# A hybrid decoder block on one core: the running sums of W_down's quarters, built in DRAM by two queues behind the weight loads

## The chip, the cores and the metric

One core of one Trainium2 chip runs the whole block. The metric is the device time of one execution in microseconds (us); lower is better. Engines: PE multiplies matrices, DVE, ACT and POOL work on vectors, SP only issues transfers. POOL can issue transfers too. A transfer issued by SP goes to the queue that the profile calls q1 (hardware), one issued by POOL to q0 (software).

## The reference, cut to what matters

```python
h = rmsnorm(x, norm_mix_pre)                                # x: 512 tokens x 1024
gq, gk, gv, gg1, gr, pu, mq, mk, mv, gates = split(h @ w_in)
ya = gla_mixer(gq, gk, gv, gg1, gr, ...) @ w_branch_a       # gated linear attention
yb = pool_mixer(pu, ...) @ w_branch_b
yc = moba_mixer(mq, mk, mv) @ w_branch_c                    # block-sparse attention
x = x + rmsnorm((sigmoid(gates) . (ya, yb, yc)) @ w_out)
h = rmsnorm(x, norm_ffn_pre)
f = (silu(h @ ffn_w_gate) * (h @ ffn_w_up)) @ ffn_w_down    # ffn_w_down: 2816 x 1024
x = x + rmsnorm(f)
```

## The kernel before

All products are made in split precision: every operand is kept as a high and a low part, and three matmuls stand for one (`mm_fm`, L212, and `mm_tm`, L221). A weight is fetched by `load` (L167) in chunks of 512 KB. `split_chunk` (L160) puts one chunk into a buffer `raw` (three of them, `NRAW`), issued by SP (L163); ACT then casts it into the high part (L164), DVE subtracts for the low part (L165), which frees the buffer. The high and the low part have four buffers each.

The order of work: the four row tiles of x are normalised and transposed, and the projection `g1r` (gate rank and half of the output gate) is done tile by tile, in an order written out by hand for DVE, ACT and PE (L370 to L423). Then come GLA's queries and keys (`gq`, `gk`), the decay, GLA's values (`gv`), the second half of the output gate (`gr`), GLA's chunks; MoBA in two halves (`mv`, `mq`, `mk`, scores and values), with the gates and the branch product `a` between; the pooling branch `b` (`pu`); branch `c`; `w_out` with its norms; the feed-forward matrices; and last the product with W_down (`product`, L930). Everything outside the hand-written stretch is put in order by a scheduler that works on a simulated timeline, with the chunks of `load` drawn ahead by a priority of 400. On its engine each instruction runs in the order so fixed, and a waiting one holds those behind it.

The last product is done by a scheme with seven products of quarters in place of eight. Four of its right-hand sides are sums of quarters of W_down. They are weights alone and are made by the transfer engines, DRAM to DRAM: for each sum, six plain copies (`sums[t, n]` from a quarter, or from an earlier sum) and six transfers that add a second quarter to it. There are 24 copies and 24 adding transfers, 512 KB each apart from four of 256 KB in either set. `background` (L149) hands out one of these 48 at each `load` other than those of `gq` and `gk`, all on POOL's queue. They have nothing to wait for but each other, so the scheduler places them as early as POOL is free. The sums are read from 777 us on.

```python
def background():
    for t, first, second in ((1, (0, 0), (0, 1)), (3, (1, 1), (0, 1)), (2, 1, (1, 1)), (4, 2, (1, 0))):
```

POOL has little else: a square root step `rs_m` for each row tile (L254), one subtraction for `g1r` (L352), clearing of buffers, some steps of GLA (L632, L636) and of MoBA (L704, L713), and the sums over the branches (L807).

Of the kernel before, what the change touches and what calls it, by code (L numbers as in the profile page):

```python
# [13 lines left out]
ALU = mybir.AluOpType  # L14
AX = mybir.AxisListType

P = 128
# [58 lines left out]
def hybrid_block(ctx: ExitStack, tc: tile.TileContext, a: dict, out: bass.AP):  # L76
    nc = tc.nc
# [16 lines left out]
    def slot(shape, name, dt=F32):  # L94
        n = int(np.prod(shape[1:]))
        if n > D or dt != F32:
            i = free_full.pop(0)
            owner[name] = (i, None, 0)
            return big.tile(shape, dt, tag=f"S{i}", name=name, bufs=1)
        if free_half:  # L100
            i, t, lo = free_half.pop(0)
        else:
            i, lo = free_full.pop(0), 0
            t = big.tile([P, 2 * D], F32, tag=f"S{i}", name=f"two_{name}", bufs=1)
            free_half.append((i, t, D))
        owner[name] = (i, t, lo)
        ap = t[:, lo:lo + n]
        names = "abcd"[:len(shape) - 1]
        if len(shape) > 2:
            ap = ap.rearrange(f"p ({' '.join(names)}) -> p {' '.join(names)}",  # L110
                              **{c: k for c, k in zip(names, shape[1:])})
        return ap
# [26 lines left out]
    chunks = [(lo, min(lo + 2, KH)) for lo in range(0, KH, 2)]  # L139

    def wq(z, c, lo, hi):

        r = (z * KH + lo) * P
        return wd[r:r + (hi - lo) * P, c * T:(c + 1) * T]

    sums = {(t, n): dram.tile([(hi - lo) * P, T], F32, name=f"sum{t}_{n}")
            for t in (1, 2, 3, 4) for n, (lo, hi) in enumerate(chunks)}

    def background():  # L149
        for t, first, second in ((1, (0, 0), (0, 1)), (3, (1, 1), (0, 1)), (2, 1, (1, 1)), (4, 2, (1, 0))):  # L150
            for n in range(len(chunks)):
                src = sums[first, n] if type(first) is int else wq(*first, *chunks[n])
                yield nc.gpsimd.dma_start(sums[t, n], src)
            for n in range(len(chunks)):
                yield nc.gpsimd.dma_start(sums[t, n], wq(*second, *chunks[n]), accum_op=ALU.add)

    behind = background()


    def split_chunk(src, kt, nf, H, L, name, eng, lead):  # L160
        with tc.high_priority(offset=lead):
            raw = wpool.tile([P, kt, nf], F32, tag="raw", name=f"raw_{name}", bufs=NRAW)
            nc.sync.dma_start(raw, src.rearrange("(k p) f -> p k f", p=P))  # L163
            S.copy(H, raw)  # L164
            (eng or V).tensor_tensor(L, raw, H.bitcast(F32), op=ALU.subtract)  # L165

    def load(src, name, eng=None, lead=LEAD, keep=False):  # L167


        if not name.startswith(("gq", "gk")):  # L170
            next(behind, None)
        K, nf = src.shape[0] // P, src.shape[1]
        kt = 4 if nf == G1W else D // nf
        out = []
        for c in range(K // kt):
            if keep:
                HL = slot([P, 2, kt, nf], f"{name}_{c}", F32R)
                h, l = HL[:, 0], HL[:, 1]
            else:
                h = wpool.tile([P, kt, nf], F32R, tag="wH", name=f"wH_{name}_{c}", bufs=NWH)  # L180
                l = wpool.tile([P, kt, nf], F32R, tag="wL", name=f"wL_{name}_{c}", bufs=NWH)
            split_chunk(src[c * kt * P:(c + 1) * kt * P, :], kt, nf, h, l, f"{name}_{c}", eng, lead)
            out.append((h, l, c * kt, kt))
        return out

    class Pair:
# [125 lines left out]
    raw = [wpool.tile([P, 4, G1W], F32, tag="raw", name=f"raw_g1r{c}", bufs=NRAW) for c in range(2)]  # L312
# [57 lines left out]
    with tc.manual_schedule(engines={E.DVE, E.Activation, E.PE}):  # L370
# [50 lines left out]
        for pair in ("HH", "HL", "LH"):  # L421
            for c in range(2):
                st_mm(3, c, pair)  # L423
    wgq = load(w_in[:, C_GQ:C_GQ + 256], "gq", None, 0)
    wgk = load(w_in[:, C_GK:C_GK + 256], "gk", None, 0)
    for t in range(NT):
        free(f"x_{t}", f"hn{t}")
# [43 lines left out]
    gq, gk = gqk[:, 0], gqk[:, 1]  # L471

    def proj_tm(dst, c, name):
        W = load(w_in[:, c:c + 256], name)
        for tp in range(2):
            ps = acc(f"{name}_{tp}")
            for j in range(2):
                mm_tm(ps[:, j * 256:(j + 1) * 256], hT, 2 * tp + j, W, 0, 256)
            dst(2 * tp, ps.rearrange("p (t f) -> p t f", t=2))
# [11 lines left out]
    for i in range(2):  # L491
        for j in range(2):
            t = 2 * i + j
# [110 lines left out]
    for c in range(NT):  # L604
        ob = side(f"o{c}")
        up = side(f"up{c}") if c < NT - 1 else None
        for p in range(2):
            n = p * 4 + c
# [7 lines left out]
        if c < NT - 1:  # L616
            for p in range(2):
                n = p * 4 + c
# [290 lines left out]
    for u in range(NF // 2):  # L909
# [5 lines left out]
        for f in range(2):  # L915
            k = 2 * u + f
# [148 lines left out]
```

## Time and profile before

| | |
|---|---|
| time, median of 3 runs | 871.37 us (870.96 to 877.25) |
| time of the profiled execution | 871.97 us |
| its span in the trace | 870.2 us |
| PE busy | 824.5 us, 95% of the span |
| DVE busy | 455.6 us, 52% |
| ACT busy | 327.0 us, 38% |
| POOL busy | 97.3 us, 11% |
| mean granted clock of PE | 0.988 |

The time of the profiled execution is its span and 1.8 us around it. A busy PE is one with a matmul in its pipeline; matmuls overlap, so that one of 512 columns lasts some 0.39 us in the rows but follows the one before by 0.23 us at the full clock.

### The profile page before, as it was taken

To read this page: it belongs to the slowest core of one execution; us is meant where nothing else is said; L and a number is where in the kernel's file an instruction comes from. 1 tells how busy PE (TensorE), PEld (TensorE's weight loads), DVE (VectorE), ACT (ScalarE), POOL (GpSimd) and SP (SyncE) were. 2 spreads that over 40 slices of the span, in tenths; PEclk is the share of its full clock that TensorE was granted. 3 is DMA by queue.
4 is the path that set the end of the run, shared out by engine and by line. 5 is a ranking of instruction groups with operands and counts; after the bars stand their busy time and mean duration, and the time that the engine had idled before them with its cause. 6 is when DMAs were issued, how large, how long until landed. Compare 5 with 4: busy or idle time off the path is not lost.

```text
span 870.2 us, 10358 instructions
## 1 busy us (share of the span) xinstructions
PE 824.5 (95%) x4082; PEld 698.6 (80%) x4082; DVE 455.6 (52%) x674; ACT 327.0 (38%) x496; POOL 97.3 (11%) x109
## 2 busy tenths in 40 slices
PE   0389989999999999999999999999999999999996
PEld 0387889888988887788888889888888888888885
DVE  1262978676647665443345563323232434586655
ACT  2144342455536542222334343222222222365543
POOL 4452300111100100121121110000000000000001
PEclk9989999999999999999999999999999999999998
DMA  8999992223132263143324242333333333268673
GB/s 289 293 236 307 275 219 74 74 72 96 51 98 82 64 201 110 52 121 97 96 97 146 97 144 76 97 96 97 97 97 97 96 98 96 85 201 284 193 210 129
DMA packets 82386, 118.39 MB, mean 136 GB/s; under 512 B 4305, under 2 KB 58338, under 8 KB 82146
## 3 DMA queue, kind: packets, MB, share of 16 engines
q1 hardware_dynamic: 74338, 94.67, 35.5%
q0 software_dynamic: 8000, 23.07, 10.9%
q8 instruction: 32, 0.52, 0.3%
q14 instruction: 16, 0.13, 0.0%
HBM read 113.53 MB, written 27.26 MB: 162 GB/s over the span
## 4 chain that ended last, share of the span: by engine, by line
PE 89%; DMA 6%; DVE 2%; SPq 1%; issue 1%; ACT 1%; DVEq 0%; POOLq 0%; POOL 0%; ACTq 0%
PE ff L218 28%; PE p L947 12%; PE pga L218 5%; PE pgb L218 5%; PE ow L229 5%; PE pgc L218 5%; DMA raw_gq<-in_w_in_dram 4%; PE gqk L218 3%; PE mv L229 3%; PE pya L218 3%; PE pu L218 3%; PE mq L218 3%; PE pyb L218 3%; PE mk L218 3%; PE pyc L218 3%; DMA raw_mv<-in_w_in_dram 2%
## 5 line engine op out<-in xcount | busy, mean ns | idle before, releaser
L218 PE MATMUL ff<-h2L,wH_ffn_w_gate 128*128 128x512 f32 (+1 forms) x192 | 71.3, 372 | 0.0
L218 PE MATMUL ff<-h2L,wH_ffn_w_up 128*128 128x512 f32 (+1 forms) x192 | 71.3, 372 | 0.0
L218 PE MATMUL ff<-h2H,wL_ffn_w_up 128*128 128x512 f32 (+1 forms) x192 | 71.3, 372 | 0.0
L218 PE MATMUL ff<-h2H,wL_ffn_w_gate 128*128 128x512 f32 (+1 forms) x192 | 71.2, 371 | 0.0
L218 PE MATMUL ff<-h2H,wH_ffn_w_gate 128*128 128x512 f32 (+1 forms) x192 | 71.2, 372 | 0.0
L218 PE MATMUL ff<-h2H,wH_ffn_w_up 128*128 128x512 f32 (+1 forms) x192 | 71.1, 371 | 0.0
L165 DVE TENSOR_TENSOR wL_ffn_w_gate<-raw_ffn_w_gate,wH_ffn_w_gate 128x1024 fp32r<-128x1024 f32 x22 | 26.9, 1225 | 78.9 <-ACT wH_ffn_w_gate L164 78.7
L939 DVE TENSOR_TENSOR wL_p<-raw_p,wH_p 128x1024 fp32r<-128x1024 f32 (+1 forms) x42 | 47.2, 1133 | 30.9 <-ACT wH_p L938 30.7
L938 ACT CAST wH_p<-raw_p 128x1024 fp32r<-128x1024 f32 (+1 forms) x42 | 41.1, 980 | 52.4 <-PE p L947 22.4
L947 PE MATMUL p<-wH_p,qs 128*128 128x512 f32 x176 | 54.7, 390 | 0.3 <-ACT two_s L1001 0.3
L165 DVE TENSOR_TENSOR wL_ffn_w_up<-raw_ffn_w_up,wH_ffn_w_up 128x1024 fp32r<-128x1024 f32 x22 | 26.9, 1225 | 41.8 <-ACT wH_ffn_w_up L164 41.7
L164 ACT CAST wH_ffn_w_up<-raw_ffn_w_up 128x1024 fp32r<-128x1024 f32 x22 | 23.2, 1053 | 68.1 <-issue 35.3
L164 ACT CAST wH_ffn_w_gate<-raw_ffn_w_gate 128x1024 fp32r<-128x1024 f32 x22 | 23.2, 1053 | 61.0 <-PE ff L218 53.1
L254 POOL TENSOR_TENSOR rs_pf<-ms_pf,half 128x1 f32<-128x1 f32 x4 | 3.4, 840 | 340.8 <-DVE ms_pf L252 340.8
L218 PEld LDWEIGHTS ff<-h2L,wH_ffn_w_up 128*128 128x128 f32 x192 | 36.2, 188 | 6.3
L218 PEld LDWEIGHTS ff<-h2L,wH_ffn_w_gate 128*128 128x128 f32 x192 | 36.2, 188 | 6.3
L218 PEld LDWEIGHTS ff<-h2H,wH_ffn_w_gate 128*128 128x128 f32 x192 | 36.1, 188 | 6.3
L218 PEld LDWEIGHTS ff<-h2H,wH_ffn_w_up 128*128 128x128 f32 x192 | 36.1, 188 | 6.3
L218 PEld LDWEIGHTS ff<-h2H,wL_ffn_w_gate 128*128 128x128 f32 x192 | 36.2, 188 | 6.2
L218 PEld LDWEIGHTS ff<-h2H,wL_ffn_w_up 128*128 128x128 f32 x192 | 36.2, 188 | 6.1
L947 PE MATMUL p<-wH_p,a 128*128 128x512 f32 x132 | 41.0, 389 | 0.0
L947 PEld LDWEIGHTS p<-wH_p,qs 128*128 128x128 f32 x176 | 33.0, 188 | 7.6 <-ACT two_s L1001 0.7
(335 smaller groups left out, 2089.4 us busy)
## 6 DMA issues: line engine op xcount, KB each, us to landing
sum<-in_ffn_w_down_dram POOLq DMA_DIRECT2D x30, 512.0 KB, 14.8
raw_ffn_w_gate<-in_ffn_w_gate_dram SPq DMA_DIRECT2D x22, 512.0 KB, 3.7
raw_ffn_w_up<-in_ffn_w_up_dram SPq DMA_DIRECT2D x22, 512.0 KB, 3.7
raw_p<-sum SPq DMA_DIRECT2D x20, 512.0 KB, 4.1
raw_p<-in_ffn_w_down_dram SPq DMA_DIRECT2D x15, 512.0 KB, 3.8
sum<-sum POOLq DMA_DIRECT2D x10, 512.0 KB, 15.6
raw_gatea<-in_w_in_dram SPq DMA_DIRECT2D x8, 512.0 KB, 3.7
raw_gateb<-in_w_in_dram SPq DMA_DIRECT2D x8, 512.0 KB, 3.6
```

The costliest lines, as they stand in the source:

```text
L164: S.copy(H, raw)
L165: (eng or V).tensor_tensor(L, raw, H.bitcast(F32), op=ALU.subtract)
L218: PE.matmul(ps, lhsT=w[:, k, f * P:(f + 1) * P], rhs=m(k0 + k, lo, hi), start=n == 0 and i == 0, stop=n == len(W) - 1 and i == len(seq) - 1)
L229: PE.matmul(ps, lhsT=m(k0 + k, lo, hi), rhs=w[:, k, c0:c1], start=first and n == 0 and i == 0, stop=last and n == len(W) - 1 and i == len( ...
L254: pows.append(G.tensor_tensor(rs, ms, half[:, 0:1], op=ALU.pow))
L938: S.copy(h, w)
L939: V.tensor_tensor(l, w, h.bitcast(F32), op=ALU.subtract)
L947: PE.matmul(ps[j], lhsT=X.part(z, k, j), rhs=w_[:, k - lo_, :], start=start and k == 0 and i == 0, stop=k == KH - 1 and i == 2, skip_group ...
```

## The change

The generator no longer issues anything by itself. At each `load` but those of `gq` and `gk`, once that load has issued its chunks, it is handed the load's last transfer and issues a pair: the copy of one part of a sum, now by SP and ordered behind that transfer on SP (`issue_after` is an order on the engine, without a wait), and the adding transfer to the same part, still by POOL, which waits until the copy has landed. The first pair comes with `gv`. The 24 pairs go with the first 24 such loads, the last with `brb10`, a weight of branch `b`. The parts and the order of the sums are as before.

```diff
             for n in range(len(chunks)):
                 src = sums[first, n] if type(first) is int else wq(*first, *chunks[n])
-                yield nc.gpsimd.dma_start(sums[t, n], src)
-            for n in range(len(chunks)):
-                yield nc.gpsimd.dma_start(sums[t, n], wq(*second, *chunks[n]), accum_op=ALU.add)
+                after = yield
+                with tc.issue_after(after.ins):
+                    nc.sync.dma_start(sums[t, n], src)
+                nc.gpsimd.dma_start(sums[t, n], wq(*second, *chunks[n]), accum_op=ALU.add)
+        while True:
+            yield
 
     behind = background()
+    next(behind)
...
-            nc.sync.dma_start(raw, src.rearrange("(k p) f -> p k f", p=P))
+            dma = nc.sync.dma_start(raw, src.rearrange("(k p) f -> p k f", p=P))
...
+        return dma
...
-        if not name.startswith(("gq", "gk")):
-            next(behind, None)
...
+        if not name.startswith(("gq", "gk")):
+            behind.send(dma)
         return out
```

## Rows read from the trace of the kernel before

**Rows 1.** The page's first part: busy time of each engine.

```profile
PE 824.5 (95%) x4082; PEld 698.6 (80%) x4082; DVE 455.6 (52%) x674; ACT 327.0 (38%) x496; POOL 97.3 (11%) x109
```

**Rows 2.** The chain that ended last: start us, us, what.

```profile
13.84 30.77 DMA raw_gq<-in_w_in_dram
...
104.79 18.14 DMA raw_mv<-in_w_in_dram
...
388.62 10.88 PE pgb L218 x48
```

**Rows 3.** Busy time by stretches; columns: stretch, length, engines, granted clock, DMA.

```profile
0.00:15.00 15.00, 0.00 (x0) 0.00 (x0) 0.80 (x3) 2.73 (x5) 6.64 (x16) 1.00 0.82 279
15.00:32.00 17.00, 6.17 (x23) 5.13 (x24) 4.43 (x8) 4.50 (x8) 8.78 (x9) 1.00 1.01 332
32.00:45.00 13.00, 4.30 (x19) 3.68 (x17) 1.52 (x3) 1.70 (x5) 4.10 (x4) 0.79 1.13 241
45.00:60.00 15.00, 13.79 (x95) 13.56 (x96) 10.54 (x24) 6.58 (x16) 10.06 (x12) 0.84 1.13 248
...
105.00:125.00 20.00, 20.00 (x135) 18.40 (x133) 14.27 (x20) 6.97 (x10) 3.45 (x4) 1.00 1.09 231
125.00:140.00 15.00, 12.25 (x93) 12.08 (x92) 14.91 (x22) 6.72 (x10) 0.00 (x0) 0.89 0.35 102
```

**Rows 4.** DMA queues and issues, 0 to 62 us: packets, MB, share; then KB each.

```profile
q0 software_dynamic: 3947, 10.29, 67.0%
q1 hardware_dynamic: 5514, 6.80, 34.9%
...
two_x<-in_x_dram SPq DMA_DIRECT2D x3, 512.0 KB, 25.8
raw_g1r<-in_w_in_dram SPq DMA_DIRECT2D x2, 544.0 KB, 26.4
...
raw_gq<-in_w_in_dram SPq DMA_DIRECT2D x2, 512.0 KB, 26.7
...
cst<-const_dram SPq DMA_DIRECT2D x1, 577.0 KB, 28.1
two_x<-in_x_dram SPq DMA_DIRECT2D x2, 256.0 KB, 3.5
two_wpre<-in_norm_mix_pre_dram SPq DMA_DIRECT2D x1, 512.0 KB, 8.8
...
ident<-const_dram SPq DMA_DIRECT2D x1, 64.0 KB, 9.6
```

**Rows 5.** Instructions in order of time, 0 to 60 us: start us, us, what.

```profile
1.27 4.66 POOL L153 DMA_DIRECT2D sum<-in_ffn_w_down_dram  x8 [0.44 <-issue]
...
16.28 0.59 POOL L254 TENSOR_TENSOR rs_m<-ms_m,half 128x1 f32<-128x1 f32 x1
16.91 1.42 DVE L332 SCALAR_TENSOR_TENSOR two_wpre<-two_x,rs_m,two_wpre 128x512 f32<-128x512 f32 x2 [10.71 <-POOL rs_m L254]
...
44.63 1.04 ACT L164 CAST wH_gq<-raw_gq 128x1024 fp32r<-128x1024 f32 x1 [10.82 <-DMA raw_gq<-in_w_in_dram]
```

**Rows 6.** Matmuls in order of time, 110 to 142 us.

```profile
116.80 1.95 PE L567 MATMUL sps<-qhat,khat 128*128 128x128 f32 x16
...
127.97 3.45 PE L567 MATMUL sps<-qhat,khat 128*128 128x128 f32 x16 [2.75 <-DVE qhat L562]
```

**Rows 7.** The page's sixth part: a load of the later stages, KB and us to landing.

```profile
raw_gatec<-in_w_in_dram SPq DMA_DIRECT2D x8, 512.0 KB, 3.6
```

**Rows 8.** In order of time, 372 to 402 us, SP's issue of a load, then ACT's cast.

```profile
374.79 7.97 SPq L163 DMA_DIRECT2D raw_gatec<-in_w_in_dram  x2
...
388.48 1.06 ACT L164 CAST wH_gatec<-raw_gatec 128x1024 fp32r<-128x1024 f32 x1 [3.94 <-issue]
```

**Rows 9.** Waits of POOL over the whole span: us in total, times, longest.

```profile
POOL eh L713 <- DVE mx L726: 102.9, 7, 42.8
...
POOL sum L155 <- DMA sum<-sum: 13.9, 9, 7.3
```

## Forecast before the run

> **What bounds the kernel now.** I read the busy times first: PE has work for 824.5 of 870.2 us [rows 1], so a change can win only where PE is idle, 45.7 us in all, or where its clock is low. The table by stretches says where that is [rows 3]. The first 60 us hold 0.00 + 6.17 + 4.30 + 13.79 = 24.26 us of PE work, so 35.7 us of idleness; 125 to 140 us holds 2.75 us; between, and from 140 us to the last product, PE is full. The rest of the idle time, some 7 us, is the tail of the last product and its norm, which the change doesn't touch.
>
> The reader should next look at the last columns of those rows: in the same stretch the transfer engines are busy all the time (share 0.82 to 1.13). The chain of waits names the transfer that PE was kept waiting for: the first chunk of `gq`, 30.77 us from issue to landing, and a chunk of `mv`, 18.14 us [rows 2], against 3.6 us for a chunk of the same size later [rows 7]. The queues tell why [rows 4]: to 62 us, SP's queue, with all that the work needs, took 34.9% of the engines' time and POOL's queue, the sums alone, 67.0%. POOL itself is a second victim: it issues eight copies from 1.27 us on, then more as they land, and the `rs_m` of the first row tile, queued behind them, runs at 16.28; DVE had waited 10.71 us for it [rows 5].
>
> **The change, part by part.**
>
> *Sums leave the start.* All 10.29 MB of POOL's queue before 62 us go [rows 4], since no pair can be issued ahead of `gv`'s last chunk. What SP's queue alone can do: 6.80 MB in 34.9% of 62 us, that is 21.6 us, 314 GB/s. Up to the first chunk of `gq` SP issues two halves of x (512 KB), the norm's weights (512), the identity (64), two `g1r` (1088), three row tiles (1536), the constants (577) and the chunk (512): 4801 KB, 4.92 MB, 15.7 us at that rate. I start the count at 1 us (POOL's first issue is at 1.27 [rows 5]). For the latency I take what a lone chunk needs beyond its own 0.52 MB / 314 GB/s = 1.7 us: 3.6 - 1.7 = 1.9 us [rows 7]. An estimate of 18.6 us for a landing that was at 13.84 + 30.77 = 44.6 us: 26.0 us earlier.
>
> *Does the work in front of it keep up?* Before, everything that ACT had ahead of that cast was done by 34 us, and it idled for 10.82 us then [rows 5]. DVE's wait began at 16.91 - 10.71 = 6.2 us, when POOL's input was there; so `rs_m` now runs at 6.2 and ends at 6.8 in place of 16.87, and the chunks of `g1r` and the row tiles land at 8 to 16 us by the same rate (1.7 MB up to the first chunk of `g1r`, 2.8 MB up to the second, 3.8 MB up to the last row tile). PE's work up to 45 us is 10.5 us [rows 3], in a chain of norm, transpose, cast, subtraction and product for two row tiles, so that it ends at some 17 to 20 us. I see the two ends close together, and take 24 us for the shift of the point that was at 44.6, two less than the transfer alone gives. From there to 60 us the rows show PE busy 13.79 of 15 us [rows 3]: that sequence stays as long as it is. *Bounds:* at best PE idles only until the first transpose (7.5 us, half of the first norm's 1.42 us behind `rs_m`, in place of the 35.7 it loses by 60 us: a gain of 28.2), and the low clock goes too (0.79 and 0.84 on 4.30 and 13.79 us of work, about 3.1 us); at worst the hand-written chain takes twice as long as I think and the point shifts by 14 us.
>
> *The wait for `mv`.* From 105 to 125 us the engines are still saturated (1.09) by the last sums; `mv` lands 18 us after its issue, DVE waits behind its cast, and the score products of GLA come late: PE idles 2.75 us and the 16 matmuls after that last 3.45 us where a like group lasts 1.95 [rows 6], at a granted clock of 0.89 over the stretch [rows 3]. Together 4.2 us. After the change some four pairs (4 MB) fall into that stage; before it was all that was left of the sums at 62 us, more than half of their 23 MB. So the load lands soon enough. But the pairs are there; I book 3 of the 4.2, and nought to 4.2 for the range.
>
> *What the pairs cost where they go.* POOL's queue moved 10.29 MB in 67.0% of 62 us, so in 41.5 us of all 16 engines, 248 GB/s [rows 4]: 2.1 us for each copy and 2.1 for each adding transfer of 512 KB. That price comes from the contended stretch, so it is high. A load of two chunks feeds some 10.9 us of PE work [rows 2] and takes twice 1.7 us; with a pair 7.6 us. The engines are then busy 70% of the time between GLA and branch `b`, not full. A copy stands behind the last chunk of its load and ahead of the next load on SP, and the next load's landing slips by the copy's 2.1 us, or 4.2 when the adding transfer runs beside it: 3.6 becomes 5.7 to 7.8 us. The cover is the three buffers: a `gatec` chunk issued at 374.79 was cast at 388.48, 13.7 us later, so it had 10 us to spare [rows 8]. Nothing is paid while that holds; if the cover were gone it would be 24 times 2.1 to 4.2 us. SP's own issue of a copy lies in time in which SP waits for a buffer to come free. Copies for the second and fourth sum read a sum made six or twelve loads earlier, some 60 us, and don't wait.
>
> *The added wait on POOL.* Each adding transfer waits in POOL's order for its copy. Before, nine such waits came to 13.9 us, the longest 7.3 [rows 9]. Behind it on POOL stand GLA's squares and powers, MoBA's scaled bias `eh` and the branch sums; DVE and then PE wait for these. For `eh` POOL waits 102.9 us in seven turns for DVE, not the other way, so there is room. I book 0 to 8 us for the whole kernel and take 1.
>
> Sum: 24 + 3 - 1 = 26 us off 871.97 of the profiled run, 846; the median lies 0.6 lower, so 845 us. Lower end: 28.2 + 3.1 + 4.2 = 35.5 off, 836. Upper end: 14 + 0 - 5, 862.
>
> By the Trainium skill, DMA: Bandwidth & Descriptors, Issuing engines are not separate DMA queues, transfers share the same 16 engines whoever issues them. By that rule handing the copies to SP wins nothing by itself. No row here tells the two apart, and the sum above takes its gain from the time at which the bytes move, not from the queue.
>
> **The rivals.**
>
> *The start is held by its order, not by bytes.* ACT runs in a fixed order, and the scheduler may put the cast of `gq`, for which ACT waited 10.82 us [rows 5], ahead of more of the hand-written steps than now. At worst all 10.5 us of PE's work ahead follow the landing at 18.6, then the 15 us: the point of 60 us moves to 44, a gain of 16, with 1 given back on the way: 856. For it: the order of ACT is made anew; against: the steps ahead are written out.
>
> *The loads behind the copies come late (slower than before).* SP's queue is where every weight comes from. If a chunk's 10 us of spare are in truth used up, because copy, adding transfer and the next loads collide, each of 24 loads is late. Slower than before from 26 / 24 = 1.1 us a load on PE's path; at the 2.1 us of a copy it is 24 times 2.1 = 50 us, 845 + 50 = 895. Against it: even at 18 us to landing, in the saturated stretch, PE lost only 2.75 us [rows 2, 3]. In the Trainium skill, DMA: Bandwidth & Descriptors, Queues, rings and completion order, an engine takes turns between queues packet by packet, but within one ring descriptors are consumed in order. By that rule a copy in SP's own queue holds the next load for its whole length, where one in POOL's would let it through by turns; it is the mechanism of this rival.
>
> *POOL's waits reach PE.* The adding transfers hold up GLA's and MoBA's steps, 18 of them up to the pooling branch. At the 13.9 / 9 = 1.5 us that one waited before [rows 9], half of it on PE's path, 13 us are given back: 858.
>
> *It doesn't do what it says.* The scheduler may let the pairs pile up early again, or PE's start hang on something that the sums hid. Then some 868 to 872.
>
> **How the numbers follow.** The forecast itself (837 to 853) 0.63; the start held by order 0.16; POOL's waits 0.10; no effect 0.06; loads late 0.05. The range 835 to 862 takes in the forecast, its bounds and nearly all of the second and third case. Within 1% is about what a measurement of this kernel can't tell from no change. Faster by over 1%: 0.63 + 0.16 + 0.10 less 0.01 = 0.88; within 1%: 0.06 and a little of the others, 0.07; slower by over 1%: 0.05.
>
> **What would show it.** Right: POOL's queue with some 11.5 MB in place of 23, SP's with 106; `rs_m` of the first tile at some 6 to 7 us; the first cast of `gq` at 17 to 20 us and PE's continuous stretch from some 36 us on; no wait for `mv`; PE busy time about as before, so that the idle time falls from 45.7 to some 20 us. Loads of the MoBA stage land after 5 to 8 us with ACT not waiting for them. Wrong: idle PE before 36 us with ACT standing at a cast (the order), ACT waiting for `raw` tiles between 70 and 350 us (loads late), DVE waiting for `eh` or `oss` (POOL).

## The result, and the profile after

The changed kernel takes 835.79 us (median of 4 runs, 834.95 to 836.22) beside 871.16 us for the kernel before on the same chip (4 runs). The ratio is 0.9578, 95% interval 0.9535 to 0.9622. The direction was forecast; the size was not: 845 had been said, with 835 to 862 for the range, and on the 871.37 us of the forecast the ratio gives 834.6, just past its fast end (the two medians alone would give 836.0, just inside it; one run of the kernel before took 877.25 us). The profiled execution is one of 836.22 us with a span of 834.4 and a granted clock of 0.998 (before: 0.988), so 35.8 us of span have to be found.

The page's busy times and queues of the changed kernel (queues: packets, MB, share of 16 engines' span):

```profile
PE 817.0 (98%) x4082; PEld 692.6 (83%) x4082; DVE 456.7 (55%) x674; ACT 328.2 (39%) x496; POOL 86.1 (10%) x85
...
q1 hardware_dynamic: 77730, 106.20, 40.4%
q0 software_dynamic: 6016, 11.54, 9.0%
```

Beside [rows 1] two things moved. PE's idle time fell from 45.7 to 834.4 - 817.0 = 17.4 us, by 28.3. And PE's *busy* time fell by 7.5 us, from 824.5 to 817.0, with the same 4082 matmuls. 28.3 + 7.5 = 35.8. The queues are as foretold: half of POOL's bytes went to SP's.

Busy time by stretches of the changed kernel (stretch, length, PE, PEld, DVE, ACT, POOL, granted clock, DMA share, GB/s):

```profile
0.00:15.00 15.00, 5.76 (x24) 5.12 (x25) 4.99 (x11) 8.05 (x17) 3.93 (x8) 1.00 0.82 310
15.00:32.00 17.00, 16.49 (x122) 15.45 (x121) 14.48 (x29) 8.57 (x18) 7.91 (x6) 1.00 0.55 161
32.00:45.00 13.00, 13.00 (x59) 10.65 (x59) 5.10 (x7) 4.48 (x6) 1.12 (x1) 1.00 0.63 185
45.00:60.00 15.00, 15.00 (x67) 11.95 (x66) 4.99 (x6) 8.87 (x11) 0.88 (x1) 1.00 0.80 191
...
100.00:125.00 25.00, 25.00 (x180) 23.54 (x180) 17.16 (x26) 7.14 (x11) 4.75 (x5) 1.00 0.64 169
125.00:140.00 15.00, 15.00 (x76) 12.68 (x75) 10.83 (x22) 6.02 (x9) 4.63 (x6) 1.00 0.57 141
```

Against [rows 3], PE is idle for 9.75 us of the first 60 in place of 35.7, the pause at 125 to 140 us is gone, and the clock is 1.00 in every row. The DMA share between 15 and 60 us is 0.55 to 0.80 where it was over 1.

The changed kernel in order of time, 0 to 36 us (start us, us, what; in brackets the idle time ahead and what ended it):

```profile
5.41 0.55 POOL L259 TENSOR_TENSOR rs_m<-ms_m,half 128x1 f32<-128x1 f32 x1 [4.57 <-DVE ms_m L257]
...
8.05 1.42 DVE L337 SCALAR_TENSOR_TENSOR two_wpre<-two_x,rs_m,two_wpre 128x512 f32<-128x512 f32 x2 [2.80 <-DMA two_wpre<-in_norm_mix_pre_dram]
...
8.86 1.97 PE L340 MATMUL tp_m<-ident,two_wpre 128*128 128x128 f32 x8 [8.86 <-DVE two_wpre L337]
...
16.17 1.07 ACT L346 CAST hTH<-tp_m 128x512 fp32r<-128x512 f32 x2 [1.08 <-PE tp_m L340]
...
18.37 1.04 ACT L168 CAST wH_gq<-raw_gq 128x1024 fp32r<-128x1024 f32 x1
...
28.70 0.40 PE L223 MATMUL gqk<-hTL,wH_gq 128*128 128x512 f32 x1
```

And the kernel before at the two points that answer to the fourth and the last of these:

```profile
45.58 1.06 ACT L341 CAST hTH<-tp_m 128x512 fp32r<-128x512 f32 x2
...
59.23 0.48 PE L218 MATMUL gqk<-hTL,wH_gq 128*128 128x512 f32 x1
```

The last row of each is the second matmul of `gq`. It comes 59.23 - 28.70 = 30.5 us earlier, which is most of the gain. A later mark, the 48 matmuls of branch `b`, shows what came between:

```profile
336.14 10.88 PE pgb L223 x48
```

In the kernel before the same piece of the chain is this one:

```profile
372.30 10.88 PE pgb L218 x48
```

So it is 36.2 us earlier. From the second matmul of `gq` to it the kernel before took 313.07 us and the changed one 307.44: another 5.6 us. Behind it 0.4 us are lost again (35.8 in all).

### The profile page after: what moved, and what is told of

Same layout as the page of the kernel before. It is cut to its first block, busy times and chain, and to the rows that moved or that the text cites. A ratio compares the mean times of both kernels' runs of the same rounds, so it can differ in the third digit from the quotient of the medians.

```text
span 834.4 us, 10373 instructions
## 1 busy us (share of the span) xinstructions
PE 817.0 (98%) x4082; PEld 692.6 (83%) x4082; DVE 456.7 (55%) x674; ACT 328.2 (39%) x496; POOL 86.1 (10%) x85
## 4 chain that ended last, share of the span: by engine, by line
PE 93%; DMA 3%; DVE 1%; ACT 1%; issue 1%; SPq 0%; POOL 0%; DVEq 0%; POOLq 0%; ACTq 0%
PE ff L223 29%; PE p L952 9%; PE pgb L223 5%; PE ow L234 5%; PE pgc L223 5%; PE pga L223 5%; PE mv L234 3%; PE gv L234 3%; PE pya L223 3%; PE mq L223 3%; PE pu L223 3%; PE pyb L223 3%; PE gqk L223 3%; PE mk L223 3%; PE pyc L223 3%; PE gr L234 1%
## 5 line engine op out<-in xcount | busy, mean ns | idle before, releaser
L223 PE MATMUL ff<-h2L,wH_ffn_w_gate 128*128 128x512 f32 (+1 forms) x192 | 71.3, 372 | 0.0
L223 PE MATMUL ff<-h2L,wH_ffn_w_up 128*128 128x512 f32 (+1 forms) x192 | 71.3, 372 | 0.0
L223 PE MATMUL ff<-h2H,wL_ffn_w_up 128*128 128x512 f32 (+1 forms) x192 | 71.3, 372 | 0.0
L156 POOL DMA_DIRECT2D sum<-in_ffn_w_down_dram x24 | 21.7, 905 | 209.1 <-DMA sum<-sum 102.5
L223 PEld LDWEIGHTS ff<-h2H,wL_ffn_w_gate 128*128 128x128 f32 x192 | 36.2, 188 | 6.3
L223 PEld LDWEIGHTS ff<-h2H,wL_ffn_w_up 128*128 128x128 f32 x192 | 36.2, 188 | 6.3
L223 PEld LDWEIGHTS ff<-h2L,wH_ffn_w_up 128*128 128x128 f32 x192 | 36.2, 188 | 6.2
L223 PEld LDWEIGHTS ff<-h2L,wH_ffn_w_gate 128*128 128x128 f32 x192 | 36.2, 188 | 6.2
```

The source lines that it names most:

```text
L223: PE.matmul(ps, lhsT=w[:, k, f * P:(f + 1) * P], rhs=m(k0 + k, lo, hi), start=n == 0 and i == 0, stop=n == len(W) - 1 and i == len(seq) - 1)
```

## The experiments

`pows[i]` are POOL's root steps `rs_m` of the row tiles 0 to 3, in the order of their making, and `issue_after(x)` puts an instruction behind `x` on its engine, without a wait on data. The kernel before was run beside each set: 870.86 us for the first four, 871.03 for the next four, 871.83 for the last.

**Is it the place in time, or the queue?** The kernel before with its transfers all left on POOL's queue, but behind the last of the four root steps:

```diff
-                yield nc.gpsimd.dma_start(sums[t, n], src)
+                with tc.issue_after(pows[3].ins):
+                    dma = nc.gpsimd.dma_start(sums[t, n], src)
+                yield dma
```

> The kernel before, with all of POOL's 48 transfers ordered behind the fourth square root step on POOL, so that they start at about 22 us; queue and bundling stay as before. If the loss lay in the start alone (bytes, or POOL's waiting steps), this comes near the changed kernel: 836 to 838 us. If the sums' bytes also cost in GLA's stage (theory of the bytes), the start is as early as in the changed kernel, but the loads of gv, gr and mv land late again: 840 to 846. If it is the queue or the pairing that matters, it stays near 871.

Measured: 843.04 us, ratio 0.9681 (0.9665 to 0.9696). Its first stretches show PE busy 6.41 of 15, 16.86 of 17, 13.00 and 15.00 us at a clock of 1.00: the whole gain of the start, and no queue was changed. The rest is lost at 100 to 140 us, where the transfers still follow closely. The chain of waits there (start us, us, what):

```profile
99.62 17.65 DMA sum<-in_ffn_w_down_dram
...
117.55 8.18 DMA sum<-sum
...
126.01 1.72 POOL sum L157 x2
127.73 1.08 POOL osq L634
```

DVE in the same stretch:

```profile
128.84 0.69 DVE L636 TENSOR_REDUCE oss<-osq 128x4 f32<-128x512 f32 x1 [10.94 <-POOL osq L634]
```

GLA's squares `osq` stand on POOL behind an adding transfer that waits for its copy; DVE waits 10.94 us for them, and PE is busy for 33.58 of 40 us there. That is the rival of POOL's waits, in a kernel that pushes the transfers together. The late loads that had been expected are there too (`gv`'s chunks take 10.9 to 12.5 us to land, `gr`'s 13.9 to 16.9), but PE is busy for 40.00 of the 40 us from 60 on: they cost nothing there, and the 843 lies in the range named for them by another cause.

**POOL's first wait, or the bytes?** The same edit with `pows[0]`: only the first root step no longer stands behind copies.

> The kernel before, with POOL's transfers ordered behind the first square root step only: the first norm no longer waits for POOL, but the bytes flow from about 6 us on. If POOL's waiting step set the start, the gain is its 10 us: 861. If the bytes set it, the bytes come 5 us later and the cast of gq with them: 866 or more.

Measured: 868.73 us, 0.9976 (0.9963 to 0.9988). Freeing POOL's first step alone gives 2 us at the end, though PE gets further than that at first: the second matmul of `gq` comes at 51.62 us in place of 59.23, 7.6 us earlier. From 60 to 140 us ACT then waits 35.0 us in all for `gk`, `gr`, `gv` and `mv`, and most of the 7.6 is lost. While the bytes move early, the loads are late, and a step that is freed only meets the next late load.

**The place in time taken away, the queue kept.** The changed kernel without its order on SP:

```diff
                 after = yield
-                with tc.issue_after(after.ins):
-                    nc.sync.dma_start(sums[t, n], src)
+                nc.sync.dma_start(sums[t, n], src)
```

> The changed kernel without the order behind the load: copies on SP's queue, adding transfers on POOL's, both as early as the scheduler can place them. SP then issues copies from some 12 us on, between the chunks of gq, gk and gv. If the time at which the bytes move decides, much of the loss returns: 850 to 865. If the queue decides, it stays at 836 to 838.

Measured: 861.01 us, 0.9886 (0.9857 to 0.9915). The copies gather ahead of `gk`. SP's issues and ACT's cast in order of time:

```profile
22.10 8.04 SPq L154 DMA_DIRECT2D sum<-in_ffn_w_down_dram  x4
...
31.67 7.85 SPq L166 DMA_DIRECT2D raw_gk<-in_w_in_dram  x1
...
64.24 1.04 ACT L167 CAST wH_gk<-raw_gk 128x1024 fp32r<-128x1024 f32 x1 [23.34 <-DMA raw_gk<-in_w_in_dram]
```

The second chunk of `gk` is issued at 31.67 and takes 32.49 us to land by the chain of waits; PE is busy for 1.76 of the 15 us from 45 on. So 25 of the 35 us hang on that one line of order. It holds the copies back to where they do no harm.

**Another queue, the same place.** The changed kernel with the copies issued by ACT, behind its cast of the load's last chunk:

```diff
-                    nc.sync.dma_start(sums[t, n], src)
+                    nc.scalar.dma_start(sums[t, n], src)
```

> The changed kernel with the copies issued by ACT, each behind the cast of the load's last chunk, the adding transfers on POOL as in the change. If the place in time decides and any queue will do that doesn't hold up others, this stays at 835 to 839, ACT paying a little for 24 issues. If SP's queue behind the loads is what wins: over 842.

Measured: 835.34 us, 0.9577 (0.9557 to 0.9597): no difference. SP's queue is not needed. The sentence in which the forecast drew on the Trainium skill, DMA: Bandwidth & Descriptors, Issuing engines are not separate DMA queues, is borne out by this run, for SP and ACT as issuers.

**The order of ACT.** After the change the cast of `gq` stands behind the casts of tile 1 and the squares of tile 3. First that order alone, in the kernel before:

```diff
-            S.copy(H, raw)
+            if name == "gq_0":
+                with tc.issue_after(squares["m3"].ins):
+                    S.copy(H, raw)
+            else:
+                S.copy(H, raw)
```

> The kernel before, with ACT's first cast of gq ordered behind the squares of the fourth row tile, where the changed kernel has it; the sums stay early. If ACT's order is what made the late landing costly, PE's full stretch starts some 10 us sooner: 861. If the bytes alone set the start, nothing changes: 868 to 871.

Measured: 874.76 us, 1.0045 (1.0028 to 1.0062). PE does 8.52 us of work between 32 and 45 us in place of 4.30, and loses it again between 60 and 100 (33.38 of 40): the row tiles go ahead, and then the weights are missing (ACT waits 16.2 us for the two chunks of `gk`). Then the reverse, the changed kernel with the cast back ahead of tile 1's:

> The changed kernel with ACT's and DVE's steps on the first chunk of gq put ahead of the casts of row tile 1, as they stood in the kernel before. The first chunk of gq lands at 17 to 18 us, the casts of tile 1 ran at 16.2. If part of what the start gained beyond the forecast came from the new place of that cast: 837 to 839. If the place makes no difference: 835.5 to 836.5.

Measured: 836.68 us, 0.9593 (0.9577 to 0.9610). ACT in order of time:

```profile
16.34 1.05 ACT L168 CAST wH_gq<-raw_gq 128x1024 fp32r<-128x1024 f32 x1 [1.12 <-DMA raw_gq<-in_w_in_dram]
17.30 1.07 ACT L346 CAST hTH<-tp_m 128x512 fp32r<-128x512 f32 x2
```

The wait for `gq` costs tile 1's cast 17.30 - 16.17 = 1.1 us, the time is some 1 us longer, between the two forecasts, and the intervals overlap.

**What do the pairs cost where they are now?** The changed kernel without any of the 48 transfers:

> The changed kernel without any sum: the 48 transfers are left out, and the four products that read sums read single quarters of the weight in their place (the numbers computed are others; the work of the engines is the same). It is the floor for any placing of the transfers. If the pairs cost nothing where they now lie: 834 to 836. If copies delay loads or POOL's waits reach PE, the difference shows it: under 832.

Measured: 834.91 us, 0.9588 (0.9572 to 0.9605), span 833.2. What the pairs still cost in the changed kernel is some 1 us, and the intervals overlap. Then one more copy, and three more, of 512 KB at each pair:

```diff
                     nc.sync.dma_start(sums[t, n], src)
+                    for e in range(1):                       # 3 in the second kernel
+                        nc.sync.dma_start(spare[t, n, e], wq(*second, *chunks[n]))
```

> The changed kernel with one more copy of the same size behind each of the 24 copies on SP's queue, into spare memory that nothing reads. If the loads have some 10 us to spare, as the forecast says, nothing changes: 836 to 838. If the loads behind copies are late as soon as a copy stands before them, each copy costs up to 2.1 us: 840 to 880.

> The changed kernel with three more copies behind each of the 24. A load then waits for four copies, 8.4 us by the contended price, close to the 10 us to spare, and the engines are asked for 3.4 + 10.5 = 13.9 us of work per 10.9 us of PE's. If the spare time is real but finite, this is where it ends: 845 to 900. If there is more to spare: 836 to 840.

Measured: 835.49 us, 0.9599 (0.9579 to 0.9620), and 855.11 us, 0.9821 (0.9800 to 0.9842). In the second the chunks land after 12.8 us, by the DMA issues of 140 to 360 us (KB each, median us to landing), and ACT stands at their casts, by the waits of that stretch (us in all, times, longest):

```profile
spare<-in_ffn_w_down_dram SPq DMA_DIRECT2D x39, 512.0 KB, 13.3
...
raw_gateb<-in_w_in_dram SPq DMA_DIRECT2D x8, 512.0 KB, 12.8
...
ACT wH_brb L173 <- DMA raw_brb<-in_w_branch_b_dram: 15.1, 2, 9.3
...
ACT wH_gateb L173 <- DMA raw_gateb<-in_w_in_dram: 11.1, 2, 9.1
```

**POOL's waits in the path.** The changed kernel with both transfers of a pair on POOL, each copy behind the adding transfer before it:

```diff
-                with tc.issue_after(after.ins):
-                    nc.sync.dma_start(sums[t, n], src)
-                nc.gpsimd.dma_start(sums[t, n], wq(*second, *chunks[n]), accum_op=ALU.add)
+                with tc.issue_after(last[0].ins):            # last: pows[3] at first
+                    nc.gpsimd.dma_start(sums[t, n], src)
+                last[0] = nc.gpsimd.dma_start(sums[t, n], wq(*second, *chunks[n]), accum_op=ALU.add)
```

> The changed kernel with both parts of a pair on POOL, each copy ordered behind the adding transfer before it, the first behind the fourth square root step. No more than about one pair is in flight, from 22 us to some 200. If it is the spreading and the start after 22 us that win, whichever queue: 835 to 839. If copies must be on SP's queue to win: over 845.

Measured: 900.70 us, 1.0342 (1.0323 to 1.0362), slower than before. Waits of 100 to 220 us, then POOL in order of time:

```profile
POOL sum L158 <- DMA sum<-sum: 71.3, 12, 8.6
...
DVE oss L641 <- POOL osq L639: 55.9, 3, 48.9
...
PE ytp L649 <- DVE osb L646: 55.6, 3, 43.7
...
164.89 0.79 POOL L157 DMA_DIRECT2D sum<-sum  x1
165.42 1.33 POOL L639 TENSOR_TENSOR osq<-osb 128x512 f32<-128x512 f32 x1
```

POOL comes to `osq` at 165.42, behind pairs whose adding transfer each waited on POOL for its copy (the first row: twelve waits, 71.3 us); DVE waits 48.9 us for it, and PE is busy for 25.57 of the 40 us from 100 on and for 24.18 of the 60 after these. So the run does not tell what POOL's queue costs; it shows what the waits cost when work for PE stands behind them.

**What does an idle PE cost?** The changed kernel with 22 clearings of a buffer on POOL ahead of the third root step, some 10 us:

```diff
+            if name == "m2":
+                for _ in range(22):
+                    with tc.issue_after(pows[1].ins):
+                        pows_hold = G.memset(hold, 0.0)
+                with tc.issue_after(pows_hold.ins):
+                    pows.append(G.tensor_tensor(rs, ms, half[:, 0:1], op=ALU.pow))
```

> The changed kernel with 22 idle clears on POOL ahead of the third square root step, some 10 us of them, so that row tile 2 comes that much later and PE stands idle in the start. If idle time is all that a late start costs, the loss is no more than those 10 us: up to 846, with the granted clock near 0.998. If PE's clock falls behind the idle stretch as it did in the kernel before, the loss is larger than the idle time that the trace shows, and the granted clock is under 0.995.

Measured: 847.11 us, 0.9712 (0.9695 to 0.9729), a span of 845.7, 11.3 us above the changed kernel's. PE's idle time is 845.7 - 818.9 = 26.8 us, 9.4 more; its busy time is 1.9 us more. By stretches:

```profile
18.00:21.00 3.00, 1.06 (x9) 0.85 (x7) 2.24 (x4) 2.22 (x5) 2.71 (x6) 1.00 0.81 270
21.00:24.00 3.00, 0.00 (x0) 0.00 (x0) 1.23 (x1) 0.43 (x1) 2.71 (x6) 0.97 0.68 189
24.00:27.00 3.00, 0.00 (x0) 0.00 (x0) 0.00 (x0) 0.00 (x0) 2.71 (x7) 0.50 0.49 164
27.00:30.00 3.00, 1.60 (x9) 1.63 (x9) 2.50 (x4) 0.47 (x1) 0.47 (x1) 0.50 0.00 0
30.00:33.00 3.00, 3.00 (x15) 3.00 (x14) 2.30 (x7) 0.70 (x2) 2.55 (x3) 0.50 0.00 0
33.00:36.00 3.00, 3.00 (x23) 3.00 (x22) 1.67 (x5) 0.84 (x2) 2.97 (x2) 0.82 0.02 5
36.00:39.00 3.00, 3.00 (x25) 2.86 (x24) 1.85 (x4) 1.00 (x3) 0.96 (x1) 1.00 0.00 0
```

The clock falls to 0.50 of 2.4 GHz, so 1.2 GHz, while PE stands, and stays there when PE is full again: 15 matmuls from 30 to 33 us, 25 in a like stretch from 36 on.

**Can the start be shorter still?** DVE's first norm waited 2.80 us for the norm's weights, so here these are issued ahead of x's first row tile:

> The changed kernel with the weights of the first norm issued ahead of the first row tile, since DVE's first norm waited for them 2.8 us, until 8.05 us. If they land 1 to 2 us sooner and the row tile no later than that: 834 to 835. If the row tile is now the late one: 836 to 837.

Measured: 835.63 us, 0.9581 (0.9565 to 0.9598): nothing. The weights are there, and the row tile is late instead; the norm starts at 8.28, not 8.05:

```profile
8.28 1.41 DVE L337 SCALAR_TENSOR_TENSOR two_wpre<-two_x,rs_m,two_wpre 128x512 f32<-128x512 f32 x2 [0.74 <-POOL rs_m L259]
```

## Why the forecast was right, and where it was short

**The cause was right.** The sums' bytes in the start were what PE waited for. Moving them in time without a change of queue gives the whole start; leaving the queue changed and taking away the order loses 25 us of the gain; another queue in the same place gives the same time; and neither POOL's first wait nor ACT's order does it by itself.

**The landing of `gq` was nearly right.** Forecast at 18.6 us; in the changed kernel it was issued at 7.92, the slower of the two chunks took 9.6 us, some 17.5 in all, and the cast at 18.37 did not wait. In the run with its cast put first ACT waited 1.12 us for it and had it at 16.34. `rs_m` was foretold at 6 to 7 us and ran at 5.41, its norm at 8.05 and not at 6.8, since the norm's weights landed late.

**The step that failed** is the one behind the landing: "From there to 60 us the rows show PE busy 13.79 of 15 us: that sequence stays as long as it is", with "PE busy time about as before" as its sign. Nearly all of the 26 us was booked as idle time. Idle time came to 28.3, a little more; but busy time fell by 7.5, booked at nought. 2.3 + 7.5 = 9.8 us is what separates the 846 forecast for the profiled run from its 836.22. By the terms of the sum the 9.8 us are these: the cast of `gq` came 44.63 - 18.37 = 26.3 us earlier where 24 stood (2.3); from it to the second matmul of `gq` the sequence took 28.70 - 18.37 = 10.33 us and not 59.23 - 44.63 = 14.60 (4.3); the stage of `mv` gave 5.6 where 3 - 1 = 2 stood (3.6); and 0.4 was lost behind.

Up to the second matmul of `gq` the kernel before is idle for 35.75 us and busy for 23.48, the changed one 9.75 and 18.95: 26.0 us of idleness and 4.5 of busy time, where 24 and 0 stood. The run with the cast of `gq` put first, also at a clock of 1.00, comes to that matmul at 30.67 after 20.57 us of busy time. So 2.9 of the 4.5 us go where the clock stays up, and the other 1.6 with the new order, in which a few matmuls fewer lie ahead. The clock of [rows 3] was read, and priced well, at 3.1 us; but it was put into the bound alone, as if it could stay low without the idle time ahead of it. Rows of the kernel before show the two one after the other (the row at 75 us is another case, told below):

```profile
39.00:42.00 3.00, 0.00 (x0) 0.00 (x0) 0.00 (x0) 0.00 (x0) 0.00 (x0) 0.59 1.13 227
42.00:45.00 3.00, 0.00 (x0) 0.00 (x0) 0.00 (x0) 0.37 (x1) 0.00 (x0) 0.50 1.19 210
45.00:48.00 3.00, 1.78 (x8) 1.79 (x8) 2.29 (x3) 2.88 (x7) 0.00 (x0) 0.50 1.22 202
48.00:51.00 3.00, 3.00 (x20) 3.00 (x20) 1.81 (x7) 1.46 (x3) 1.06 (x2) 0.70 1.16 209
...
75.00:78.00 3.00, 3.00 (x10) 2.37 (x10) 0.81 (x2) 2.99 (x3) 2.02 (x3) 0.65 0.99 303
...
129.00:132.00 3.00, 3.00 (x17) 3.00 (x16) 2.96 (x6) 1.59 (x3) 0.00 (x0) 0.55 0.07 25
```

In the run with an idle PE 9.4 us of idleness cost 11.3: there a pause cost its length and slow time behind it.

What the clock by itself was worth in the kernel before is not shown. Eight of its 27 runs beside the experiments have a granted clock of 0.993 to 0.998 on record, and they took 870.69 to 873.97 us, no less than the other nineteen at 0.981 to 0.991, which took 868.34 to 872.65. And in the run with POOL's first step freed, 7.6 us gained at `gq` came to 2 at the end. As long as the loads are late, PE may lose in waiting what it gains in speed. So 28.3 and 7.5 say how two traces differ; they are not the worth of two separate causes.

**The sequence got shorter** by its order as well. The forecast let everything follow the cast of `gq`. The scheduler put tile 1's cast ahead of it, at 16.17 (45.58 before, 29.4 us), and what follows tile 1's cast up to the second matmul of `gq` took 12.53 us in place of 13.65. With the old order put back the cast of `gq` comes at 16.34, 28.3 us earlier, and from it to that matmul it is 14.33 us, at a clock of 1.00: there the sequence does stay about as long as it was, and the start still gives 28.6 us where 24 stood. The order made anew was a rival there, priced as a loss; it went the other way, and is worth some 1 us at the end by the run that put it back (the intervals overlap).

**The wait for `mv`** went, as booked, and more with it. Booked were 3 of 4.2 us, with 1 given back to POOL: 2. Measured were 5.6: the 2.75 us of idle PE and the 1.5 of slow matmuls behind it [rows 6], and, in no step, some 1.6 at 73.3 to 76.9 us, where the matmuls of `gk` follow one another by 0.43 us in the kernel before and by 0.23 later. Against these 5.85 us the changed kernel idles for 0.2 in the same piece. At 73 us PE had been full; why the clock fell is open, and with it whether its going belongs to the change. The three are read from one trace each.

**POOL's waits** grew and cost nothing. POOL's waits for copies over the whole span of the changed kernel (us in all, times, longest):

```profile
POOL sum L156 <- DMA sum<-sum: 102.5, 12, 14.6
POOL sum L156 <- DMA sum<-in_ffn_w_down_dram: 97.4, 11, 19.1
```

Against the 13.9 us of [rows 9], with 2.7 more in two waits that the forecast left out, that is 199.9. Almost none of it reaches PE: without any transfer the kernel is only some 1 us faster. The rival is real where pairs gather ahead of GLA (6.7 us of span above the changed kernel behind the last root step, 65 us with all pairs on POOL). What keeps it away here is the pairing with `gv` and later loads, which spreads the transfers from 37 to 324 us.

**Loads behind the copies** land a little later, and it costs nothing. DMA issues between 40 and 330 us in the changed kernel (KB each, median us to landing):

```profile
raw_gatea<-in_w_in_dram SPq DMA_DIRECT2D x8, 512.0 KB, 4.8
...
raw_mv<-in_w_in_dram SPq DMA_DIRECT2D x4, 512.0 KB, 3.8
```

The same with the copies in ACT's queue:

```profile
raw_gatea<-in_w_in_dram SPq DMA_DIRECT2D x8, 512.0 KB, 4.2
...
raw_mv<-in_w_in_dram SPq DMA_DIRECT2D x4, 512.0 KB, 4.0
```

And without any transfer of the sums:

```profile
raw_gatea<-in_w_in_dram SPq DMA_DIRECT2D x8, 512.0 KB, 3.4
```

From 5.7 to 7.8 us had been said for a chunk behind a copy; over all chunks of `gatea` it is 4.8, and 6.0 at most, and `mv`, which was at 18.14 [rows 2], is at 3.8. A likely reason stands in SP's order of time: between 133 and 315 us it issues the next load 2.4 to 7.9 us behind a copy, since that load needs a free buffer, and half of the copies have landed after 4.9 to 5.5 us. Much of a copy is over when the load starts. The spare of 10 us [rows 8] held for one copy more and was gone with three, at 12.8. The rule that stood beside this rival (the Trainium skill, DMA: Bandwidth & Descriptors, Queues, rings and completion order) would let the loads land sooner with the copies in a queue of their own. Here `gatea` gains 0.6 us by that and `mv` loses 0.2: of the 1.4 us by which `gatea` lies above the run without sums, 0.8 are left with the copies in another queue. At this load the order in the ring decides nothing that the time shows (835.79 and 835.34 us).

No kernel tried clearly beats the changed one: it and three of its variants lie at 835.34 to 835.79 us, and with no transfers at all the time is 834.91.

## What to carry to other kernels

Transfers that nobody waits for still have a place in time: put them where loads have room (here one copy behind each load, with up to one more free of charge), not where an engine happens to be free. An order without a wait is enough, and which queue takes them may not matter, as long as no wait for them stands ahead of work on the engine that issues them (65 us with all pairs on POOL). And when a gain is counted from PE's idle time, look at the granted clock of the busy time behind each pause as well: here it was the part that the forecast booked at nothing.

## What was not expected of the hardware

The clock at 73 us is told above. Just ahead of that fall lie eight small products of the decay, `lg`, at 70.22 and 72.37 us; but the same eight follow each other from 51.09 us in the changed kernel, and stand in the same two groups, at 73.48 and 75.63, in the run with ACT's cast behind the squares, and the granted clock stays at 1.00 behind both.

From 8 to 18 us, where in the changed kernel SP's queue has the engines nearly to itself, the stretch reads:

```profile
8.00:18.00 10.00, 8.39 (x44) 7.50 (x45) 6.64 (x12) 7.35 (x17) 4.54 (x3) 1.00 1.06 385
```

So the engines moved 385 GB/s at a full share there, where with the sums beside the loads they moved 332 and less [rows 3], and where the forecast had worked out 314 from [rows 4]. In slices of 3 us the kernel before comes to 412 GB/s too (21 to 24 us), and falls to 202 (45 to 48 us). So over longer stretches the engines moved less while the sums ran beside the loads; which property of the sums does that was not tried.
